# A gated residual block on one core: two head pairs and a quarter of the frames per step of the recurrence, r, k, v by way of DRAM, grams of two heads in turn

## The chip, the core and the metric

The kernel runs on one core of a Trainium2 chip. The metric is device time in microseconds of one execution; the runs of the kernel before took 2218.48 us in the median (2216.34 to 2221.33). The core has five engines that work beside each other, each in its own order: TensorE (PE; its weight loads are listed as PEld), VectorE (DVE), ScalarE (ACT), GpSimd (POOL) and SyncE (SP), which here issues all transfers. TensorE writes to PSUM, from where VectorE and ScalarE fetch its results.

## The reference

One layer over 1024 frames of 1024 channels, cut to what matters:

```
h    = RMSNorm(x);  P = h @ W_in             # r | k | v | glu | gate logits
r, k, v: each mixed with the frame before
w, a, g: low-rank functions of h             # decay, learning rate, gate
kk = normalised (k * k_k) per head;  k = k * (1 + (a - 1) * k_a)
# 16 heads of 64 channels, state S (64 x 64) per head, frame by frame
S_t = S_{t-1} diag(w_t) - (S_{t-1} kk_t) (kk_t a_t)^T + v_t k_t^T
o_t = S_t r_t
A    = (GroupNorm(o) + bonus(r, k, v)) * g
C    = swish(LayerNorm(causal depthwise conv, 31 taps, of the glu))
y    = sigmoid(gA) * (A @ W_A) + sigmoid(gC) * (C @ W_C)
x    = x + y @ W_out;  x = x + relu(RMSNorm(x) @ W1)^2 @ W2;  out = RMSNorm(x)
```

## The kernel before, in words

All data lies with channels on the partitions, 128 at a time, and frames along the free dimension, in halves of 512 (SEG). A large product is done as three products of float32r parts (high x high, high x low, low x high), 128x512 each; a unit of the combined projection is 48 of them. The weights come by DMA into `raw` and are split into `whi` (ScalarE) and `wlo` (VectorE or GpSimd).

**The recurrence** is done by chunks of 64 frames. Within a chunk it is matrix algebra; from chunk to chunk the state is handed on. Two heads of 64 channels fill the 128 partitions: a head pair p, of eight. A step i of 16 is one head pair and one half of the frames, 8 chunks. The parts of a step are generators:

- `prep` (L695) loads the decay (`sg`) and learning rate (`ta`), makes the scaled keys `bk`, the probes `pr` and the bonus. r, k, v of the pair are taken from SBUF, where the evacuation of the projection (`u_rkv`, L651) left them, three buffers each.
- `front` (L797), once for each four chunks: transposes `bk`, then makes the gram products `pg` of `bk` with `pr`: four for the first head (partitions 0 to 63), a tick, four for the second (64 to 127). ScalarE and VectorE copy them out, masked, to `lt`, `pl` and `mr`. The PSUM buffers `pg`, `pt`, `pv`, `pi`, `px` and so on share two banks.
- `invert` (L842): the inverse of I - L of each chunk, diagonal blocks of 16 by substitution on GpSimd after a way through DRAM (`scr_l`, `scr_x`, `scr_z`, `xz`), then blocks of 32 and 64 by small products (`pi`, `px`, `pt`, `pz`).
- `v_tm` (L774): transposes v into `sav` and `stv`, which then hold v beside places for the state.
- `chain` (L934): the chunks one after another, three groups of products a chunk, one a tick. First group: `pc` from `stv` and `pl`, and `po` from `stv` and `pr`; VectorE copies `pc` to `rsb`. Second group: `pc` from `rsb` and the inverse z; VectorE copies it to `sav`. Third group: `pc` from `sav` and `bkt`, and `po` from `sav` and `mr`; VectorE makes the next chunk's state, `pc` times the decay `wc` plus `stw`, where `stw` is the old state times the decay, made by ScalarE.
- `group_norm` (L986), after the chain of the step; its result goes to `a_d` in DRAM.

**The order.** Everything in this stage is traced by one loop of ticks, 24 (NT) for a step. At each tick every live generator is taken one stage further, then large products are traced until a running price of TensorE's work (`mm_price`) reaches the tick's number times 1.8 us (`large`), then some operations of the convolution on VectorE. `PLAN` (L1111) says at which tick of which step a generator starts. While the loop runs, TensorE, VectorE, ScalarE, GpSimd and SP keep exactly the order in which they are traced. The large products come from a queue: r, k, v of a pair when the last pair's are used, the glu, then the 16 gate units.

**The tail.** After the loop, 16 products of `g2t` with `tg` (the gate of A) follow, with up to 1.7 us of leftover gate products traced before each, and then the products with W_A, the merge and the feed-forward part. These last read nothing that the change touches.

Of the kernel before, what the change touches and what calls it, by code (L numbers as in the profile page):

```python
# [17 lines left out]
P = 128  # L18
T = 1024
NK = 8  # L20
SEG = 512
NSEG = 2
# [72 lines left out]
def tile_hybrid_block(ctx: ExitStack, tc: tile.TileContext, xT, win, wap, wcp, wop, wf1, wf2,  # L95
# [3 lines left out]
    class Ordered:  # L99
        """While on, the instructions of an engine keep the order in which they are traced;  # L100
        work: how long they take, in ns."""
# [58 lines left out]
    z_d = [dtile(f"z_d{i}", [P, T]) for i in range(NK)]  # L160
    al_d = [dtile(f"al_d{i}", [P, T]) for i in range(NK)]
    bn_d = [dtile(f"bn_d{i}", [P, T]) for i in range(NK)]
# [192 lines left out]
    def pick():  # L355
        """The first of the queue whose time has come."""
# [26 lines left out]
    def rms_scale(acc, eps):  # L383
        """acc [128, SEG], per-partition partial sums of squares, becomes 1/sqrt(mean + eps) on all partitions."""
# [1593 lines left out]
```

## Time and profile before

| | |
|---|---|
| runs, median (lowest to highest) | 2218.48 us (2216.34 to 2221.33) |
| profiled execution, its span | 2220.0 us |
| TensorE busy | 2075.3 us, 93%, 12806 records |
| VectorE busy | 1617.9 us, 73%, 2781 instructions |
| ScalarE busy | 1120.3 us, 50%, 2102 instructions |
| GpSimd busy | 898.0 us, 40%, 1026 instructions |
| transfers | 224.87 MB, mean 101 GB/s |

The profiled execution is one run, 1.5 us longer than the median of the others. A busy share is a mean over stages with different limits, so the stage that is changed is read by itself. TensorE's records of matrix products are pipelined and their ends are modelled: a busy time holds overlap, and the distance from one start to the next says what a product costs. A product of float32 operands has two records, so "x8" in a row is four products.

### The profile page before, as it was taken

What the parts mean: (1) busy time and instruction counts of PE and PEld (TensorE: products, weight loads), DVE (VectorE), ACT (ScalarE), POOL (GpSimd) and SP (SyncE); (2) the same over time, 40 slices, a digit from 0 to 9 for tenths busy, and PEclk for the clock granted to TensorE, in tenths of its full rate; (3) what the DMA queues carried; (4) which work ended last, traced back from release to release, by engine and by line L of the source; (5) the groups of instructions that cost most, each with busy time, mean ns of one, the idle gap of its engine ahead of it and who ended that gap; (6) DMA issues with size and microseconds to landing.
All of it is one profiled execution on the core that took longest, in us unless ns stands there. A gap on an engine that the chain in (4) does not pass through costs nothing. (4 is left out here: it accounts for less than half of the span.)

```text
span 2220.0 us, 35280 instructions
## 1 busy us (share of the span) xinstructions
PE 2075.3 (93%) x12806; PEld 1554.3 (70%) x12806; DVE 1617.9 (73%) x2781; ACT 1120.3 (50%) x2102; POOL 898.0 (40%) x1026
## 2 busy tenths in 40 slices
PE   6999999999999999999989989799899998889897
PEld 4757666767676666676666778577688876667686
DVE  8435889869778888898484987979432249998865
ACT  7454555555555555654323753455555555333323
POOL 4103333333333333342112245665545456566641
PEclk8999999999999999999999999999899999999999
DMA  5243222222222222232254355242433334233212
GB/s 180 90 158 79 62 73 53 80 65 78 78 66 79 72 81 72 74 87 82 70 178 159 128 170 163 95 137 93 169 105 114 105 106 151 91 95 105 85 49 76
DMA packets 223358, 224.87 MB, mean 101 GB/s; under 512 B 113488, under 2 KB 131408, under 8 KB 223184
## 3 DMA queue, kind: packets, MB, share of 16 engines
q1 hardware_dynamic: 223184, 222.62, 32.3%
q8 instruction: 101, 1.65, 0.3%
q14 instruction: 73, 0.60, 0.1%
HBM read 155.96 MB, written 66.60 MB: 100 GB/s over the span
## 5 line engine op out<-in xcount | busy, mean ns | idle before, releaser
L114 POOL TENSOR_TENSOR wlo<-raw,whi 128x512 fp32r<-128x512 f32 x258 | 369.4, 1434 | 698.9 <-ACT whi L114 640.1
L114 PE MATMUL g<-hhi,whi 128*128 128x512 f32 x912 | 402.9, 442 | 0.0
L114 PE MATMUL g<-hhi,wlo 128*128 128x512 f32 x912 | 363.4, 398 | 2.1 <-POOL wlo L114 1.5
L114 PE MATMUL g<-hlo,whi 128*128 128x512 f32 x912 | 364.8, 400 | 0.0
L114 ACT ACTIVATE whi<-raw 128x512 fp32r<-128x512 f32 x328 | 204.5, 625 | 222.4 <-PE g L114 73.0
L114 PEld LDWEIGHTS g<-hhi,whi 128*128 128x128 f32 x912 | 173.1, 190 | 52.4 <-issue 6.0
L114 PE MATMUL x<-place,whi 128*128 128x512 f32 x608 | 195.5, 403 | 14.8 <-DVE cmean L114 7.8
L114 PE MATMUL x<-a,whi 128*128 128x512 f32 x544 | 177.2, 408 | 33.3 <-ACT c L114 11.3
L114 PE MATMUL g<-place,whi 128*128 128x512 f32 x624 | 198.8, 399 | 7.6 <-ACT place L114 4.1
L114 PEld LDWEIGHTS g<-hhi,wlo 128*128 128x128 f32 x912 | 174.4, 191 | 44.5 <-POOL wlo L114 2.4
L114 PE MATMUL g<-a,whi 128*128 128x512 f32 x624 | 196.9, 397 | 5.7 <-DVE c L114 3.3
L114 PEld LDWEIGHTS g<-hlo,whi 128*128 128x128 f32 x912 | 174.1, 191 | 26.6 <-issue 1.9
L114 DVE TENSOR_TENSOR c<-c,g 128x512 f32<-128x512 f32 (+1 forms) x131 | 84.6, 650 | 94.8 <-PE g L114 94.6
L114 PEld LDWEIGHTS x<-a,whi 128*128 128x128 f32 x544 | 105.2, 196 | 63.0 <-ACT c L114 12.7
L114 PEld LDWEIGHTS x<-place,whi 128*128 128x128 f32 x608 | 115.1, 192 | 48.1 <-issue 6.2
L114 POOL TENSOR_TENSOR wlo<-s,whi 128x512 fp32r<-128x512 f32 x72 | 107.5, 1495 | 100.1 <-ACT whi L114 91.8
L114 PEld LDWEIGHTS g<-place,whi 128*128 128x128 f32 x624 | 118.2, 190 | 38.6 <-ACT place L114 5.0
L114 PEld LDWEIGHTS g<-a,whi 128*128 128x128 f32 x624 | 117.7, 190 | 35.7 <-DVE c L114 4.6
L114 POOL TENSOR_TENSOR tmpb<-lb,xb 64x15 f32<-64x15 f32 (+7 forms) x240 | 110.2, 459 | 79.3 <-DMA lb<-scr_l 63.2
L114 ACT ACTIVATE stw<-stv,wc 64x64 f32<-64x64 f32 x240 | 82.6, 344 | 97.7 <-DVE stv L114 94.2
L114 PE MATMUL g<-a,wlo 128*128 128x512 f32 x312 | 123.4, 396 | 5.6 <-POOL wlo L114 5.2
L114 PE MATMUL g<-place,wlo 128*128 128x512 f32 x312 | 123.6, 396 | 1.6 <-POOL wlo L114 1.6
(286 smaller groups left out, 4327.6 us busy)
## 6 DMA issues: line engine op xcount, KB each, us to landing
raw<-wf SPq DMA_DIRECT2D x128, 256.0 KB, 2.8
raw<-win SPq DMA_DIRECT2D x124, 256.0 KB, 3.1
f_d<-c SPq DMA_DIRECT2D x56, 256.0 KB, 2.0
fl<-f_d SPq DMA_DIRECT2D x46, 256.0 KB, 2.9
c<-f_d SPq DMA_DIRECT2D x18, 256.0 KB, 3.3
xt<-xT SPq DMA_DIRECT2D x16, 256.0 KB, 5.3
ga_d<-gt SPq DMA_DIRECT2D x16, 256.0 KB, 2.1
z_d<-za SPq DMA_DIRECT2D x16, 256.0 KB, 2.0
```

Of the source, the lines that this page charges most:

```text
L114: ins = f(*a, **k)
```

## The change

A step now takes two head pairs (`e` = 0, 1) and a quarter of the frames (QF = 256, four chunks). There are again 16 steps and 24 ticks a step, and the tiles of a step keep their sizes, since 2 x 256 frames stand where 512 stood. The state is handed on four times a step, for both pairs at once, two ticks from group to group.

- `u_rkv` stores r, k, v to DRAM; `prep` fetches them by quarters (`fetched`), one buffer each.
- Operations with a factor per channel are split in two, one for each pair: the square of k, `kk`, `ta`, `rkk`, the last one of the group norm, and the `a_d` store.
- In `front`, the gram products of both heads are traced in turn into two PSUM buffers taken at once.
- In `chain`, the state's old part enters the third group's sum by a product of the identity with `stv`, so ScalarE's `stw` goes, and VectorE multiplies the sum by the decay.
- The first two pairs' r, k, v and the first glu unit are made before the loop; later pairs' units come due at fixed ticks.

```diff
+    rkv_d = {n: [dtile(f"{n}_d{i}", [2, P, T]) for i in range(NK // 2)] for n in "rkv"}
-        rp = st.enter_context(tc.tile_pool(name="rp", bufs=3))
+        rp = st.enter_context(tc.tile_pool(name="rp", bufs=1))
...
-                    RKV[which, NSEG * p + s] = t
+                    sync.dma_start(rkv_d[which][p // 2][p % 2][:, s * SEG : (s + 1) * SEG], t)
+                    made.add((which, p, s))
...
+        def quarter(d, i):
+            return d[i // 4].rearrange("e p t -> p e t")[:, :, (i % 4) * QF : (i % 4 + 1) * QF]
+        def block(e, c):
+            return 4 * e + c
+        def fetched(which, i):
+            pp, u = divmod(i, 4)
+            need(which, 2 * pp, u // 2)
+            need(which, 2 * pp + 1, u // 2)
+            t = rp.tile([P, SEG], F32, tag=which, name=which)
+            sync.dma_start(two(t), quarter(rkv_d[which], i))
+            return t
...
-            k = RKV["k", i]
+            k = fetched("k", i)
             sg, ta = t2k("sg"), t2k("ta")
-            sync.dma_start(sg, z_d[p][:, sl])
-            sync.dma_start(ta, al_d[p][:, sl])
+            sync.dma_start(two(sg), quarter(z_d, i))
+            sync.dma_start(two(ta), quarter(al_d, i))
+            yield
             sq = t2k("sq")
-            act.activation(sq, k, AF.Square, scale=v("kk", p))
+            for e, p in enumerate(P2):
+                act.activation(two(sq)[:, e], two(k)[:, e], AF.Square, scale=v("kk", p))
...
-            for h in range(2):
-                rows = slice(64 * h, 64 * h + 64)
-                pg = mp.tile([P, 4, P], F32, tag="m", name="pg")
-                for j in range(4):
-                    pe.matmul(pg[:, j, :], bk[rows, 4 * q + j, :, :].rearrange("p a t -> p (a t)"),
+            pgs = [mp.tile([P, 4, P], F32, tag="m", name="pg") for h in range(2)]
+            for j, b in enumerate(blocks):
+                for h, rows in enumerate((H0, H1)):
+                    pe.matmul(pgs[h][:, j, :], bk[rows, b, :, :].rearrange("p a t -> p (a t)"),
                               pr[rows, j, :, :].rearrange("p a t -> p (a t)"), start=True, stop=True)
-                yield
...
+            for c in range(4):
+                q, cc = divmod(c, 2)
...
+                for e in pairs:
+                    for h in range(2):
+                        pe.matmul(ps1[hr[h], e], Q["pl"][:, h, 2 * e + cc, :], stv[:, h, 2 * e + cc, :],
+                                  start=True, stop=True)
+                rs = sp.tile([P, 2, 64], F32, tag="rsb", name="rsb", bufs=2)
+                dve.tensor_copy(rs, ps1)
...
-                    stw = sp.tile([P, 64], F32, tag="stw", name="stw", bufs=2)
-                    for h in range(2):
-                        act.activation(stw[hr[h]], Q["stv"][hr[h], h, j, :], AF.Copy,
-                                       scale=wc[hr[h], c, 0:1])
...
+                if not (u == 3 and c == 3):
+                    for e in pairs:
+                        for h in range(2):
+                            pe.matmul(ps3[hr[h], e], ident[:, 64 * h : 64 * h + 64], stv[:, h, 2 * e + cc, :],
+                                      start=True, stop=False)
+                            pe.matmul(ps3[hr[h], e], Q["bkt"][:, 2 * e + cc, 64 * h : 64 * h + 64],
+                                      sav[:, 2 * e + cc, 64 * h : 64 * h + 64], start=False, stop=True)
...
                     for h in range(2):
-                        dve.scalar_tensor_tensor(out=nstv[hr[h], h, nj, :], in0=ps3[hr[h]],
-                                                 scalar=wc[hr[h], c, 0:1], in1=stw[hr[h]],
-                                                 op0=ALU.mult, op1=ALU.add)
+                        dve.tensor_tensor(out=nstv[hr[h], h, nc_:4:2, :], in0=ps3[hr[h]],
+                                          in1=wc[hr[h], c:8:4, :].to_broadcast([64, 2, 64]), op=ALU.mult)
...
-        PLAN = [(1, 2, prep), (24, 0, group_norm), (15, 2, front0), (24, 2, front1), (35, 2, v_tm), (29, 2, invert)]
+        PLAN = [(0, 2, prep), (24, 0, group_norm), (14, 2, front0), (24, 2, front1), (34, 2, v_tm), (28, 2, invert)]
...
+        while ("v", 1, 1) not in made:
+            large(pe.work + TICK)
+            conv_ops(2, dve.work + TICK * DSHARE)
```

What this makes of TensorE's order is shown at three places. The first is the gram products of one front, with buffer numbers. Before, each head's four stand together, into one buffer, with a group of the chain between the heads:

```order
L114 MATMUL l_10937<-hsh_10842,bonr_156 128x512
L114 MATMUL l_10937<-hsl_10844,bonr_156 128x512
L114 MATMUL pg_10942<-pr_10885,bk_10789 128x128 x4
L114 MATMUL pc_10950<-stv_10194,pl_9869 64x64 x2
L114 MATMUL po_10492<-pr_9844,stv_10194 64x64 x2
L114 MATMUL pg_10965<-pr_10885,bk_10789 128x128 x4
```

After, the heads' eight alternate between two buffers:

```order
L115 MATMUL l_5705<-hsh_5662,bonr_156 128x512
L115 MATMUL l_5705<-hsl_5664,bonr_156 128x512
L115 MATMUL pg_5709<-pr_5665,bk_5299 128x128
L115 MATMUL pg_5710<-pr_5665,bk_5299 128x128
L115 MATMUL pg_5709<-pr_5665,bk_5299 128x128
L115 MATMUL pg_5710<-pr_5665,bk_5299 128x128
L115 MATMUL pg_5709<-pr_5665,bk_5299 128x128
L115 MATMUL pg_5710<-pr_5665,bk_5299 128x128
L115 MATMUL pg_5709<-pr_5665,bk_5299 128x128
L115 MATMUL pg_5710<-pr_5665,bk_5299 128x128
```

Numbers 5709 and 5710 are the two heads' buffers: what was two groups of four is one of eight.

The second place is the third group of a chunk on TensorE, with what stands around it. Before, two products into `pc` and two into `po`:

```order
L114 MATMUL g<-hhi,wlo 128x512
L114 MATMUL pc<-sav,bkt 64x64 x2
L114 MATMUL po<-mr,sav 64x64 x2
L114 MATMUL l<-hsh,bonr 128x512
L114 MATMUL l<-hsl,bonr 128x512
```

After, for two pairs (`cst` holds the identity):

```order
L115 MATMUL g<-hhi,wlo 128x512
L115 MATMUL pc<-stv,cst 64x64
L115 MATMUL pc<-sav,bkt 64x64
L115 MATMUL pc<-stv,cst 64x64
L115 MATMUL pc<-sav,bkt 64x64
L115 MATMUL pc<-stv,cst 64x64
L115 MATMUL pc<-sav,bkt 64x64
L115 MATMUL pc<-stv,cst 64x64
L115 MATMUL pc<-sav,bkt 64x64
L115 MATMUL po<-mr,sav 64x64 x4
```

The product of the identity and the one with `bkt` that follows it go to the same half of the partitions; then comes the other half. The first and second groups have four products of each kind where they had two.

The third place is the tail on TensorE, from the last large products on h (`hhi`, `hlo`) to the first with W_A (`a`). Before, nine large products stand between one product of `g2t` and the next, for the first nine:

```order
L114 MATMUL g<-hlo,whi 128x512
L114 MATMUL g<-hhi,wlo 128x512
L114 MATMUL g<-tg,g2t 128x512
L114 MATMUL g<-hhi,whi 128x512
L114 MATMUL g<-hlo,whi 128x512
L114 MATMUL g<-hhi,wlo 128x512
```

After, there are none left:

```order
L115 MATMUL g<-hhi,wlo 128x512
L115 MATMUL l<-hsh,bonr 128x512
L115 MATMUL l<-hsl,bonr 128x512
L115 MATMUL g<-tg,g2t 128x512 x15
L115 MATMUL cm<-cmean_12306,cst 128x512
L115 MATMUL g<-tg,g2t 128x512
L115 MATMUL g<-a_12331,whi 128x512 x2
```

In the whole order, the runs of small products between large ones number 393 before and 245 after; behind the last product of the chain stand 269 large products on h before, 81 after.

## Rows read from the trace of the kernel before

**Rows 1.** Windows: length, busy us of PE, PEld, DVE, ACT, POOL, clock, DMA share, GB/s.

```profile
0.00:231.00 231.00, 207.90 (x924) 148.83 (x924) 130.41 (x239) 124.05 (x210) 50.14 (x74) 0.94 0.39 126
231.00:1135.60 904.60, 871.56 (x7681) 619.84 (x7680) 742.99 (x1582) 492.79 (x1045) 314.72 (x580) 0.99 0.27 73
1135.60:1218.60 83.00, 78.40 (x301) 57.19 (x300) 49.05 (x69) 28.77 (x46) 15.91 (x12) 0.98 0.61 199
1218.60:2220.00 1001.40, 917.44 (x3906) 728.40 (x3904) 695.48 (x894) 474.72 (x804) 517.19 (x360) 0.97 0.34 113
```

**Rows 2.** Timeline of PE, chain groups: start us, us, operation, records, idle before.

```profile
515.84 0.39 PE L114 MATMUL g<-hhi,wlo 128*128 128x512 f32 x1
516.16 0.33 PE L114 MATMUL pc<-rsb,z 64*64 64x64 f32 x4
516.42 0.50 PE L114 MATMUL g<-hhi,whi 128*128 128x512 f32 x1
...
531.77 0.39 PE L114 MATMUL g<-hhi,wlo 128*128 128x512 f32 x1
532.09 0.34 PE L114 MATMUL pc<-sav,bkt 128*64 128x64 f32 x4
532.26 0.29 PE L114 MATMUL po<-mr,sav 128*64 128x64 f32 x4
532.47 0.50 PE L114 MATMUL g<-hhi,whi 128*128 128x512 f32 x1
532.81 0.40 PE L114 MATMUL g<-hlo,whi 128*128 128x512 f32 x1
533.05 0.39 PE L114 MATMUL g<-hhi,wlo 128*128 128x512 f32 x1
...
533.73 0.39 PE L114 MATMUL g<-hhi,wlo 128*128 128x512 f32 x1
534.05 0.34 PE L114 MATMUL pc<-stv,pl 128*64 128x64 f32 x4
534.32 0.33 PE L114 MATMUL po<-pr,stv 64*64 64x64 f32 x4
534.58 0.49 PE L114 MATMUL g<-hhi,whi 128*128 128x512 f32 x1
```

**Rows 3.** Timeline of PE, the gram products of one head and what follows.

```profile
519.04 1.16 PE L114 MATMUL pg<-pr,bk 64*128 64x128 f32 x8
520.13 0.34 PE L114 MATMUL pc<-stv,pl 128*64 128x64 f32 x4
```

**Rows 4.** Timeline of PE, products of the inverse, both heads in turn.

```profile
504.76 1.15 PE L114 MATMUL pi<-xz,lm 64*64 64x64 f32 x32
505.84 0.34 PE L114 MATMUL pc<-sav,bkt 128*64 128x64 f32 x4
506.00 0.29 PE L114 MATMUL po<-mr,sav 128*64 128x64 f32 x4
506.59 0.69 PE L114 MATMUL px<-lm,xz 32*32 32x32 f32 x32 [0.30 <-ACT lm L114]
```

**Rows 5.** Tile sg: ns min/median/max, first and last start us, landing.

```profile
L114 SPq DMA_DIRECT2D sg<-z_d x14: 423/464/730, 224.5 to 960.2; - x14
L114 DVE TENSOR_TENSOR_SCAN cum<-scanmask,sg x14: 1214/1215/1225, 238.9 to 969.7; 128x512 f32<-128x512 bf16 x14
DMA to landing us min/median/max: 3.6/4.7/6.1
```

**Rows 6.** Timeline of PE, the tail: last product of the chain, first with W_A.

```profile
1135.29 0.34 PE L114 MATMUL po<-mr,sav 128*64 128x64 f32 x4
...
1186.68 1.02 PE L114 MATMUL g<-tg,g2t 128*128 128x512 f32 x2
...
1218.61 1.03 PE L114 MATMUL g<-a,whi 128*128 128x512 f32 x2
```

More of the change, by code (lines that the diff above doesn't have):

```diff
@@ L748, in prep @@
             rkk = t2k("rkk")
-            dve.scalar_tensor_tensor(out=rkk, in0=r, scalar=v("rk", p), in1=k2, op0=ALU.mult, op1=ALU.mult)
+            for e, p in enumerate(P2):
+                dve.scalar_tensor_tensor(out=two(rkk)[:, e], in0=two(r)[:, e], scalar=v("rk", p),
+                                         in1=two(k2)[:, e], op0=ALU.mult, op1=ALU.mult)
             yield
@@ L767, in prep @@
             yield
-            need("v", i)
             bn = rkk
-            dve.tensor_tensor(out=bn, in0=ps, in1=RKV["v", i], op=ALU.mult)
+            dve.tensor_tensor(out=bn, in0=ps, in1=E["v"], op=ALU.mult)
             yield
-            sync.dma_start(bn_d[p][:, sl], bn)
+            sync.dma_start(quarter(bn_d, i), two(bn))
         def v_tm(i):
-            vv = RKV["v", i]
+            vv = D[i]["v"]
             pv = mp.tile([P, 4, P], F32, tag="m", name="pv")
@@ L778, in v_tm @@
                 pe.transpose(pv[:, w, :], vv[:, w * P : (w + 1) * P], ident)
-            done.add(("v", i))
             yield
@@ L939, in chain @@
             hr = [H0, H1]
+            pairs = range(2)
             po = op.tile([P, NCH, 64], F32, tag="o", name="po")
[L941 to L942 removed]
+            for c in range(4):
+                q, cc = divmod(c, 2)
                 Q = E["q"][q]
[L944 removed]
+                stv, sav = Q["stv"], Q["sav"]
+                pc = chp.tile([P, 3, 2, 64], F32, tag="c", name="pc")
                 ps1, ps2, ps3 = pc[:, 0], pc[:, 1], pc[:, 2]
[L946 to L958 removed]
@@ L959, in chain @@
+                yield
+                yield
+                for e in pairs:
+                    for h in range(2):
+                        pe.matmul(ps2[hr[h], e], z[hr[h], block(e, c), :], rs[hr[h], e], start=True, stop=True)
+                for h in range(2):
+                    dve.tensor_copy(sav[0:64, cc:4:2, 64 * h : 64 * h + 64], ps2[hr[h]])
                 yield
-                for h in range(2):
-                    pe.matmul(ps2[hr[h]], z[hr[h], c, :], rs[hr[h]], start=True, stop=True)
@@ L962, in chain @@
-                dve.tensor_copy(Q["sav"][0:64, j, 0:64], ps2[0:64])
-                dve.tensor_copy(Q["sav"][0:64, j, 64:128], ps2[64:128])
                 yield
-                if not last:
-                    for h in range(2):
-                        pe.matmul(ps3[hr[h]], Q["bkt"][:, j, 64 * h : 64 * h + 64],
-                                  Q["sav"][:, j, 64 * h : 64 * h + 64], start=True, stop=True)
-                    if c < NCH - 1:
-                        nq, nj = divmod(c + 1, 4)
+                if not (u == 3 and c == 3):
+                    for e in pairs:
+                        for h in range(2):
+                            pe.matmul(ps3[hr[h], e], ident[:, 64 * h : 64 * h + 64], stv[:, h, 2 * e + cc, :],
+                                      start=True, stop=False)
+                            pe.matmul(ps3[hr[h], e], Q["bkt"][:, 2 * e + cc, 64 * h : 64 * h + 64],
+                                      sav[:, 2 * e + cc, 64 * h : 64 * h + 64], start=False, stop=True)
+                    if c < 3:
+                        nq, nc_ = divmod(c + 1, 2)
@@ L1015, in group_norm @@
             bn = sp.tile([P, SEG], F32, tag="gns", name="gnb")
-            sync.dma_start(bn, bn_d[p][:, sl])
+            sync.dma_start(two(bn), quarter(bn_d, i))
             yield
@@ L1019, in group_norm @@
             yield
-            dve.scalar_tensor_tensor(out=o, in0=o, scalar=v("lxg", p), in1=bn, op0=ALU.mult, op1=ALU.add)
+            for e in range(2):
+                dve.scalar_tensor_tensor(out=two(o)[:, e], in0=two(o)[:, e], scalar=v("lxg", 2 * (i // 4) + e),
+                                         in1=two(bn)[:, e], op0=ALU.mult, op1=ALU.add)
             yield
-            sync.dma_start(a_d[p][:, sl], o)
+            for e in range(2):
+                sync.dma_start(a_d[2 * (i // 4) + e][:, (i % 4) * QF : (i % 4 + 1) * QF], two(o)[:, e])
         convs = []
@@ L1089, in conv, with need @@
             done.add(("c_d", p))
-        queue.append((passed(), [u_rkv(0, "k"), decay_and_a, u_rkv(0, "r"), u_rkv(0, "v"), gate_lora]))
-        for p in range(NK):
-            if p:
-                i = NSEG * p + NSEG - 1 - 3
-                queue += [(passed((n, i)), [u_rkv(p, n)]) for n in "krv"]
-        queue += [(lambda p=p: p == 0 or ("conv", p - 1) in done, glu_units(p)) for p in range(NK)]
+        queue.append((passed(), [u_rkv(0, "k"), u_rkv(1, "k"), decay_and_a] + glu_units(0) +
+                      [u_rkv(e, x) for x in "rv" for e in range(2)] + [gate_lora]))
+        tick = [0]
+        for pp in range(1, NK // 2):
+            for j, (x, e) in enumerate((x, e) for x in "krv" for e in range(2)):
+                due = NT * (4 * pp - 4) + 15 * j
+                queue.append((lambda due=due: tick[0] >= due, [u_rkv(2 * pp + e, x)]))
+        queue += [(lambda p=p: ("conv", p - 1) in done, glu_units(p)) for p in range(1, NK)]
         queue += [(passed(), [gate_unit(n, (1,) if n < EARLY else (0, 1))]) for n in range(2 * NK)]
         advance(8)
-        def need(which, i):
-            while (which, i) not in RKV:
+        def need(which, p, s):
+            while (which, p, s) not in made:
                 next(G)
```

98 lines of the change are left out of this document (51 added, 47 removed).

## The prediction

> **What bounds the kernel now.** I read the table of stages first, because the change touches one stage only. The span falls into four pieces: a start, the recurrence, a short tail, and the feed-forward part [rows 1]. In the recurrence, 904.6 us long, TensorE is busy for 871.6 us, so 33.0 us are idle. VectorE is busy 743 us (82%), ScalarE 493 us, GpSimd 315 us, and the DMA engines 27%. TensorE bounds this stage and the others almost as closely. Nothing else may be said to bound it as long as VectorE's share stays below TensorE's. So I look for what the change does to the time that TensorE needs, and then for what it does to the 33 us.
>
> A busy TensorE hides two prices. The timeline of TensorE shows them as start-to-start distances, which I trust more than modelled ends. Large products (128x512) follow one another every 0.24 us (532.81 to 533.05) [rows 2]. Each excursion into small products costs more than the products do. I take the distance from the last large product before it to the first one after it, less 0.235 us:
>
> - the second group of a chunk, two products (pc from rsb and z): 516.42 - 515.84 - 0.235 = 0.345 us [rows 2];
> - the third, four products (pc from sav and bkt, po from mr and sav): 532.47 - 531.77 - 0.235 = 0.465 us;
> - the first, four products in two shapes (pc from stv and pl, po from pr and stv): 534.58 - 533.73 - 0.235 = 0.615 us.
>
> The first large product after an excursion then takes 0.34 us instead of 0.235 us (532.47 to 532.81) [rows 2], so leaving costs 0.105 us per excursion. The gram products of one head, four of them, take 520.13 - 519.04 = 1.09 us, or 0.27 us each [rows 3]. Sixteen 64x64 products that alternate between the two heads (pi) take 505.84 - 504.76 = 1.08 us, or 0.0675 us each [rows 4]. That is a quarter of a gram product at half its columns, thus twice as fast per column: two heads in different halves of the array's rows run together there.
>
> **The change part by part.** There are 16 steps before and after, of 24 ticks each. Before, a step has 8 chunks of one pair, so 128 chunk turns; after, 4 chunks of two pairs, so 64 turns of twice the products.
>
> *Fewer, longer groups.* The price of one more pair of products within a group is 0.135 us (eight pairs of pi in 1.08 us) [rows 4] to 0.17 us (the distance from pc to po in the third group) [rows 2]; I take 0.14 us, the value for two heads side by side. Per turn:
> first group 0.615 + 2 x 0.14 = 0.895 us against 2 x 0.615 = 1.23: 0.335 us less;
> second group 0.345 + 0.14 = 0.485 against 0.69: 0.205 us less;
> third group: another po pair (0.14), and eight products into pc where there were two, since the product of the identity with stv takes the place of ScalarE's stw. Were all eight to pair, they would add 3 x 0.14 = 0.42 us. Were none to, a product of 64 columns alone is half a gram product (0.135 us), and they would add 8 x 0.135 - 0.14 = 0.94 us. In the new order two products for the same half of pc follow each other, then two for the other half, so only neighbours across the border can pair: I take 0.61 us, between the two. The group then costs 0.465 + 0.14 + 0.61 = 1.215 us against 0.93: 0.285 us more.
> Sum: 0.255 us less per turn, x 64 = 16 us less (28 us less to 5 us more).
>
> *Fewer exits.* In the program's order TensorE has 393 excursions before and 245 after. 148 x 0.105 = 15.5 us less. That the other groups (px, pt of the inverse, the transposes) now stand partly alone is in this count.
>
> *Grams in pairs.* 256 gram products in 64 groups of four: 64 x 1.09 = 70 us. After, 32 groups of eight that alternate between heads. If two run together, a group of eight costs what four cost now, 1.09 us: 35 us less. If not, nothing is gained; a loss would need a price for changing the bank, and no row has one. The heads stand in different halves of the rows as in pi, but unlike there both write all 128 partitions, so the rows do not decide it. I take the pairing, because the nearest rows are those of pi, and keep 0 as the other end.
> The Trainium skill, TensorEngine Tiling (Array Packing), section Gotcha 1: PSUM Pressure, says that row tiles must write to different banks and cannot use one bank at once. The new order meets that, and the old one could not have gained by alternation alone; no row of before shows two row halves over the same columns.
>
> *The identity products' weight loads.* In the third group of before, two products over all 128 rows, loads included, take 0.17 us [rows 2], so their loads hide.
> The Trainium skill, TensorE: Matmul & The Clock Gate, Part 3, The mechanism, says that weight loads overlap running products only where the row groups differ, else only by way of the background buffer; here all eight share all rows. By that rule the eight would not pair at all, the 0.61 us become 0.94 us, and the sum below shrinks by 60 x 0.33 = 20 us. The row speaks against it.
>
> *VectorE and ScalarE.* The chain's VectorE operations halve in number (five a turn) and double in width; three per step are split in two. ScalarE loses stw. Neither engine is the bound, so I cost this at nothing; the cover is TensorE's 871.6 us against 743 us. It would cost something only if VectorE's work came above some 840 us.
>
> *Stalls.* A group of the chain now has two ticks for the answer of VectorE, where it had one. Of the 33.0 us idle I take 10 us as gone (0 to 20). Something new comes late: in about nine places px now follows pi with no product between. Today px starts 506.59 - 505.84 = 0.75 us after pi, with the third group between them and still 0.30 us of waiting for ScalarE's lm [rows 4]. Alone it waits the 0.75 us: 9 x 0.75 = 7 us more.
>
> *r, k, v through DRAM.* 48 stores and 48 loads of 256 KB, and one more a_d store per step, all behind each other on SP's queue with the weight loads. The first reader is ScalarE's square of k, one tick (904.6/384 = 2.4 us) after the load; behind it on ScalarE stands bkt's copy, which frees a PSUM buffer, and TensorE waits for that. Today SP issues the load of sg 9.5 to 14.4 us before VectorE's scan reads it, which stands two ticks (4.7 us) behind in the order [rows 5]. So SP runs 5 to 10 us ahead, plus the one tick, 7 us at the least, against 4.7 us from issue to landing (6.1 us at most). I cost it at nothing; that lead hides it.
>
> *Start and tail.* The first two pairs' r, k, v are made before the loop: the same large products, earlier. They are then missing at the end: after the last product of the chain there are 81 large products on h instead of 269. Before, that tail takes 1218.61 - 1135.29 = 83.3 us [rows 6], of which 269 x 0.235 = 63.2 us are large products. After, 19.0 us of them are left beside the other 20 us. The group norm of the last step must pass under these; the filler is thinner, the fifteen tg products stand in a row, and the last ones wait for it. I put that at 3 us (0 to 44).
>
> Sum: -16 - 15.5 - 35 - 10 + 7 + 3 = -66.5 us. On the profiled span of 2220.0 us this gives 2153.5 us. The median of the runs shown, 2218.48 us, stands 1.5 us under that span, so I predict 2152 us. The bounds of the terms without the tail's far end, which is a rival, reach from -28 - 15.5 - 35 - 20 + 7 + 0 = -91.5 us to +5 - 15.5 - 35 + 0 + 7 + 10 = -28.5 us, grams paired.
>
> **The rivals.**
>
> *The grams don't pair.* For it: both write the same columns of the array, which no row shows done at once. Against it: pi. Then 35 us fewer are saved: 2187 us.
>
> *The tail is not covered.* If the last group norm takes as long as now, the tail stays 83.3 us although 44 us of its large products went elsewhere: 2152 + 41 = 2193 us. Against it: the group norm of before was paced by large products and by VectorE's last convolution, which now ends inside the loop.
>
> *More is saved.* The eight products pair fully and most stalls go, the lower bound above: 2220 - 91.5 - 1.5 = 2127 us.
>
> *Slower: the loads come late.* If the stores of r, k, v hold SP back (a store waits for VectorE, and everything on the queue behind it waits too) and its lead is lost, each of the three loads of a step is seen whole by its reader: 16 x 3 x 4.7 = 226 us, so 2152 + 226 = 2378 us. From 66.5/16 = 4.2 us of TensorE idle per step on the kernel is slower than before, which is about one load seen whole. Against it: SP's lead [rows 5].
>
> **How the numbers follow.** Forecast 0.62, grams unpaired 0.13, tail uncovered 0.09, more saved 0.09, loads late 0.07. The forecast's own range is 2135 to 2175 us. The range 2120 to 2198 us takes in the unpaired grams, the open tail and the larger gain; the loads and a combination of losses are left out. A difference of 0.2% (4.4 us) is what a measurement of this kernel can tell from none. Faster 0.89: all but the loads, and a little of the two middle rivals together. Same 0.04, slower 0.07.
>
> **What would show it.** Right: gram groups of eight in about 1.1 us, their records starting in pairs; the three groups of a turn near 0.9, 0.5 and 1.2 us; the last product of the chain near 1110 us instead of 1135 us (1218.6 - 66.5 - 42 for the tail); the tail near 40 us; the feed-forward part unchanged at 1001 us. Wrong: gram groups of 2.1 us; third groups above 1.5 us; TensorE idle behind ScalarE's square of k or behind PSUM copies in every step; large idle time among the tg products.

## The result: slower by 1.6%, and the profile after

The changed kernel takes 2255.4 us (median; 2249.4 to 2259.3 in four runs), the kernel before 2217.4 us beside it: ratio 1.0156, 95% interval 1.0127 to 1.0186. The forecast was 2152 us, range 2120 to 2198. It was wrong in sign.

The first view to read is the same table of stages as in [rows 1], for the kernel after (length, busy time of PE, PEld, DVE, ACT, POOL, granted clock, DMA share, GB/s):

```profile
0.00:305.20 305.20, 276.69 (x1233) 203.20 (x1233) 173.64 (x313) 141.47 (x240) 58.77 (x83) 0.96 0.38 128
305.20:1198.40 893.20, 792.00 (x8031) 599.65 (x8030) 660.71 (x1270) 444.75 (x848) 311.48 (x567) 0.94 0.34 96
1198.40:1247.30 48.90, 38.10 (x124) 22.70 (x120) 28.12 (x42) 19.57 (x30) 10.22 (x8) 0.90 0.71 239
1247.30:2247.60 1000.30, 918.31 (x3906) 729.62 (x3904) 699.01 (x894) 474.53 (x803) 518.74 (x360) 0.97 0.34 113
```

Start, tail and feed-forward part are nearly as forecast. The start is 74 us longer, for 309 large products that now stand there (the prediction gave it no number of its own). The tail takes 48.9 us (forecast about 42), the last stage 1000.3 us, 1.1 us less than before. The loss is in the second row. Forecast for it: 805 us (last product of the chain near 1110). Measured: 893.2 us. TensorE is busy for 792.0 us, 17 us more than the 775 us that 805 less 30 of idle time leave; and it idles for 101.2 us where 33.0 us stood before and 30 were forecast. Its mean granted clock is 0.94 instead of 0.99: the clock records add up to 116 us at half speed (1.2 GHz) in this stage, against 20.5 us before.

The unit prices of the prediction hold, away from the waits. The timeline of TensorE after, with the second group (`pc<-rsb,z`), eight grams and the third group, answers to [rows 2, 3]:

```profile
537.48 0.40 PE L115 MATMUL g<-hhi,wlo 128*128 128x512 f32 x1
537.81 0.45 PE L115 MATMUL pc<-rsb,z 64*64 64x64 f32 x8
538.19 0.50 PE L115 MATMUL l<-hsh,bonr 128*128 128x512 f32 x1
538.53 0.40 PE L115 MATMUL l<-hsl,bonr 128*128 128x512 f32 x1
538.85 1.16 PE L115 MATMUL pg<-pr,bk 64*128 64x128 f32 x16
539.95 0.49 PE L115 MATMUL g<-hhi,whi 128*128 128x512 f32 x1
...
541.22 0.40 PE L115 MATMUL g<-hhi,wlo 128*128 128x512 f32 x1
541.55 0.34 PE L115 MATMUL pc<-stv,cst 128*64 128x64 f32 x4
541.72 0.29 PE L115 MATMUL pc<-sav,bkt 128*64 128x64 f32 x4
541.83 0.34 PE L115 MATMUL pc<-stv,cst 128*64 128x64 f32 x4
541.95 0.33 PE L115 MATMUL pc<-sav,bkt 128*64 128x64 f32 x4
542.07 0.45 PE L115 MATMUL po<-mr,sav 128*64 128x64 f32 x8
542.45 0.49 PE L115 MATMUL g<-hhi,whi 128*128 128x512 f32 x1
```

Eight grams take 1.10 us to the next start, as four did before. The second group costs 538.19 - 537.48 - 0.235 = 0.475 us (forecast 0.485), the third 542.45 - 541.22 - 0.235 = 0.995 us (forecast 1.215), the first 0.855 us (forecast 0.895, a stretch not shown). So away from the half clock the work fell by as much as the sum said, and a little more (in numbers: an estimate, under *The clock* below). What came back is waiting, and time at half clock. TensorE's three longest waits in the recurrence, first before, then after (what was waited for, us in total, times, longest):

```profile
PE pc L114 <- DVE stv L114: 13.7, 26, 1.2
PE pi L114 <- DMA xz<-scr_x: 6.6, 8, 1.6
PE pc L114 <- DVE sav L114: 4.0, 7, 1.2
```

```profile
PE pi L115 <- DMA xz<-scr_x: 29.6, 13, 6.1
PE pt L115 <- DVE bk L115: 19.1, 10, 2.8
PE pc L115 <- DVE stv L115: 18.2, 16, 2.1
```

The largest is pi, the first product of the inverse, for the load of xz. One such place on TensorE's timeline answers to [rows 4]; these rows follow one another without a gap in the list:

```profile
679.16 1.16 PE L115 MATMUL pg<-pr,bk 64*128 64x128 f32 x16
682.20 0.45 PE L115 MATMUL pc<-stv,pl 128*64 128x64 f32 x8 [1.88 <-DVE stv L115]
682.58 0.45 PE L115 MATMUL po<-pr,stv 64*64 64x64 f32 x8
686.42 0.44 PE L115 MATMUL pi<-xz,lm 64*64 64x64 f32 x2 [3.39 <-DMA xz<-scr_x]
687.34 1.97 PE L115 MATMUL pi<-xz,lm 64*64 64x64 f32 x30 [0.47 <-DMA xz<-scr_x]
689.24 0.79 PE L115 MATMUL g<-hhi,whi 128*128 128x512 f32 x1
689.83 0.63 PE L115 MATMUL g<-hlo,whi 128*128 128x512 f32 x1
```

TensorE waits 1.88 us for stv, then 3.39 us for xz. When it resumes, 15 products of pi take 1.97 us where 16 took 1.15, and the second large product behind them starts 0.59 us after the first instead of 0.34 [rows 2]: the clock is at half. The windows of the kernel after around it show that (same columns as above):

```profile
660.00:683.60 23.60, 19.45 (x173) 14.60 (x172) 20.21 (x39) 17.89 (x33) 18.13 (x32) 1.00 0.31 89
683.60:690.50 6.90, 3.60 (x35) 2.89 (x35) 2.00 (x6) 0.60 (x1) 0.00 (x0) 0.51 0.87 239
```

What pi waits for is a path outside TensorE. SP's queue in the same step (start of each transfer, its issue in us):

```profile
655.85 1.28 SPq L115 DMA_DIRECT2D scr_l<-lt  x2
...
658.98 0.59 SPq L115 DMA_DIRECT2D lb<-scr_l  x1
...
681.03 0.58 SPq L115 DMA_DIRECT2D scr_x<-xb  x1
...
683.62 1.27 SPq L115 DMA_DIRECT2D xz<-scr_x  x2
```

lt goes to DRAM and comes back as lb, GpSimd substitutes until 681.0, xb goes to DRAM and comes back as xz: 30.6 us from 655.85 to pi at 686.42. From the second store of lt to pi it is 33.1 us in the mean of the 16 steps after (29.1 to 36.9) and 32.9 us before (29.5 to 35.4); to the last xz load's issue, 30.0 and 29.5 us. Its length did not change. In the program's order pi stands 14 ticks behind the last lt, before and after. Before, 14 ticks are 14 x 2.36 = 33 us, just enough. With the forecast stage of 805 us a tick is 2.1 us, and 14 are 29 us. At that pace TensorE would arrive some 4 us early in each of 16 steps (an estimate from mean ticks). The experiments test this.

### The profile page after: what moved, and what is told of

Its sections match the earlier page's. It is cut to its first block, busy times and chain, and to the rows that moved or that the text cites. A ratio compares the mean times of both kernels' runs of the same rounds, so it can differ in the third digit from the quotient of the medians.

```text
span 2247.6 us, 35965 instructions
## 1 busy us (share of the span) xinstructions
PE 2025.1 (90%) x13286; PEld 1555.2 (69%) x13286; DVE 1561.5 (69%) x2517; ACT 1080.3 (48%) x1920; POOL 899.2 (40%) x1018
## 3 DMA queue, kind: packets, MB, share of 16 engines
q1 hardware_dynamic: 253648, 247.79, 35.1%
## 5 line engine op out<-in xcount | busy, mean ns | idle before, releaser
L115 PE MATMUL g<-hhi,whi 128*128 128x512 f32 x912 | 392.2, 430 | 0.2 <-ACT whi L115 0.2
L115 PE MATMUL g<-hhi,wlo 128*128 128x512 f32 x912 | 370.6, 406 | 2.9 <-POOL wlo L115 1.2
L115 PE MATMUL g<-hlo,whi 128*128 128x512 f32 x912 | 371.3, 407 | 0.0
L115 PEld LDWEIGHTS g<-hhi,whi 128*128 128x128 f32 x912 | 178.0, 195 | 47.5 <-issue 4.3
L115 PE MATMUL x<-place,whi 128*128 128x512 f32 x608 | 195.0, 402 | 12.6 <-DVE cmean L115 7.8
L115 POOL TENSOR_TENSOR tmpb<-lb,xb 64x15 f32<-64x15 f32 (+7 forms) x240 | 109.2, 455 | 46.0 <-DMA lb<-scr_l 29.5
L115 PE MATMUL x<-place,wlo 128*128 128x512 f32 x304 | 121.7, 400 | 0.9 <-POOL wlo L115 0.9
```

The source lines that it names most:

```text
L115: ins = f(*a, **k)
```

## Experiments

**Two theories.** *Short ticks*: the ticks got shorter, the inverse's path did not, so TensorE waits at pi, and its clock falls. *Loads*: the stores of r, k, v hold SP's queue, k comes late, and all behind it. For the second speaks that ScalarE's square of k does wait after:

```profile
ACT sq L115 <- DMA k<-k_d: 23.0, 6, 4.8
```

**k early.** In the kernel after, k's load is issued about ten ticks sooner, into a second buffer:

```diff
-            k = fetched("k", i)
+            k = K.pop(i) if i in K else fetched("k", i)
...
             probe(0)
+            if i + 1 < NK * NSEG:
+                K[i + 1] = fetched("k", i + 1)
```

> The kernel after, with one change: the load of k for the next step is issued at the end of this step's preparation (stage 14, about ten ticks before its first reader, into a second buffer) instead of one tick ahead. Theory of the loads (the stores of r, k, v hold SP's queue back, so ScalarE's square of k waits and all that hangs on it comes late): ScalarE's wait of 27.6 us on k goes below 4 us, TensorE's wait of 19.1 us on pt from VectorE's bk goes below 6 us, and the time falls by 15 to 30 us, to 2225 to 2240 us. Theory of the short ticks (TensorE's tick got shorter than paths that are counted in ticks, such as the inverse, and these stay): ScalarE's wait goes too, but TensorE meets the other waits sooner (pi on xz, 30.3 us, grows), and the time stays within 10 us of 2255 us.

Measured: 2252.2 us, ratio to before 1.0147 (1.0119 to 1.0175), not to be told from after. The recurrence takes 901.7 us. The wait for k is gone from ScalarE, and TensorE's waits are what they were:

```profile
PE pi L115 <- DMA xz<-scr_x: 30.5, 13, 6.2
PE pc L115 <- DVE stv L115: 20.6, 16, 2.6
PE pt L115 <- DVE bk L115: 18.0, 10, 2.8
```

The loads theory falls for k: its wait is real, and taking it away gains nothing that the runs can tell.

**pi two ticks later.** In the kernel after, pi and the inverse's products behind it stand 16 ticks behind lt:

```diff
-W_XZ = 2
+W_XZ = 4
```

> The kernel after, with the products on the inverse's blocks (pi and what follows it) two ticks later in the order, 16 instead of 14 ticks after the second half of lt. Theory of the short ticks: TensorE's 30.3 us of waits for xz go below 8 us, since 16 ticks of 2.1 to 2.3 us are 34 to 37 us and the path takes 31 to 34 us; the time falls by 15 to 30 us, to 2225 to 2240 us. Theory of the loads: the waits for pt and stv, which it puts behind late loads of k, stay, and TensorE's idle time only moves there: within 10 us of 2255 us.

Measured: 2198.5 us, ratio 0.9907 (0.9877 to 0.9938): 57 us less than after, twice what I expected, and faster than before. The stage's row, then TensorE's waits:

```profile
308.40:1142.70 834.30, 770.47 (x8064) 582.55 (x8064) 650.48 (x1269) 448.16 (x852) 306.13 (x567) 0.98 0.36 103
```

```profile
PE pt L115 <- DVE bk L115: 13.4, 10, 2.4
PE pc L115 <- DVE stv L115: 11.8, 13, 1.9
PE pi L115 <- DMA xz<-scr_x: 11.3, 8, 3.7
```

58.9 us of the stage are gone: 37.4 us of idle time (101.2 to 63.8), of which pi's wait is 18.3, and 21.5 us of busy time, with the time at half clock down from 116 to 41 us. The same products run; they run fast more of the time. That is the part that I had not expected. And ScalarE's wait for k, 23.0 us in after, is gone too, though k is loaded no sooner here:

```profile
ACT sq L115 <- DMA k<-k_d: 1.0, 1, 1.0
```

The late k was thus not the stores' doing alone, since the same stores stand on SP's queue here; it came and went with pi's place.

**Grams cheaper in the order's price list.** In the kernel after:

```diff
+        if r.dtype == F32 and l.shape[0] <= 64 and width(l) == 128:
+            n *= 2.7
-        if r.dtype == F32:
+        elif r.dtype == F32:
```

> The kernel after, with the price that the order counts for a gram product cut from 213 to 144 ns (the trace has 1.16 us for eight), so that about 75 more large products stand within the recurrence, most of them just behind the grams, and only a handful is left behind it. Theory of the short ticks and of the clock that goes with them: the ticks with grams become longer, TensorE idles less (101 us to 70 or less) and its clock is granted at half for fewer than 116 us (70 or so); 17 us of work move from the tail into the recurrence, and the time falls by 20 to 40 us, to 2215 to 2235 us. Theory of the loads: the idle time stays at 90 to 100 us, the recurrence is longer by the 17 us that the tail is shorter, and the time stays within 10 us of 2255 us, or is longer where the tail is now uncovered.

Measured: 2273.4 us, 18 us slower than after. What the theory of short ticks said here failed, and of the two theories the other came nearer (idle time of 90 to 100 us, a longer time where the tail is uncovered). This run does not speak for short ticks; the runs that vary the place of pi, above and below, do. The stage takes 919.0 us, idle 100.5 us, half clock 119.5 us; pi's wait for xz is 39.8 us. The added products came on top and filled no idle time: the 14 ticks hold only one of a step's two groups of grams, and the path was itself somewhat longer in this run (means of 16 steps from the second scr_l to the last xz load's issue: 30.9 us against 30.0). The tail, with 42 products instead of 124, still takes 45.7 us: it is set by its own waits, not by its products.

**Paired grams alone, in the kernel before.** The loop over heads moves inside the loop over blocks, and both banks are taken at once:

```diff
-                for j in range(4):
-                    pe.matmul(pg[:, j, :], bk[rows, 4 * q + j, :, :]...
-                yield
+            for j in range(4):
+                for h, rows in enumerate((H0, H1)):
+                    pe.matmul(pgs[h][:, j, :], bk[rows, 4 * q + j, :, :]...
+            yield
```

> The kernel before, with one part of the change alone: the gram products of both heads in one tick, alternating between two PSUM banks. If pairing is worth what it seemed (32 groups more of four at 1.09 us that vanish, 35 us) and nothing new waits: 2183 us. Theory of the short ticks: half or more of it comes back as waits for the inverse's path (pi on xz, 6.6 us before, 15 to 25 us here): 2195 to 2210 us. Rival, the two PSUM buffers: with both taken at once the next product into them waits for VectorE's and ScalarE's reads, and the time is not below 2217 us.

Measured: 2217.4 us, ratio 0.9997 (0.9979 to 1.0015). The stage's row:

```profile
231.50:1130.70 899.20, 842.41 (x7681) 592.96 (x7680) 742.80 (x1584) 493.24 (x1045) 317.68 (x580) 0.99 0.27 73
```

TensorE is 29 us less busy than before (871.6) and 24 us more idle (56.8 against 33.0). Pairing is real, and nearly all of it is waited away. The time is the one that the rival of the two PSUM buffers gave (not below 2217 us), and a part is of its kind: pi waits 7.3 us for mr, VectorE's read that frees the buffer. The rest is not: TensorE's waits for sav rose from 4.0 to 17.1 us, and pi waits 8.7 us for xz. The path to the last xz load's issue is itself longer here, 32.2 us in the mean against 29.5; why is not settled.

**The substitution in fewer ticks, pi where it was**, and **with pi two ticks later**. N_SUB, the steps of GpSimd's substitution per tick, goes from 2 to 4; W_XZ to 6 in the first run (shown) and to 8 in the second, so that pi stands 14 and 16 ticks behind lt.

```diff
-N_SUB = 2
+N_SUB = 4
-W_XZ = 2
+W_XZ = 6
```

> The kernel after, with GpSimd's 15 substitution steps of the inverse handed out in three ticks instead of seven (N_SUB 4), and the four ticks put behind the loads of xz, so that pi stays 14 ticks behind lt. Less of GpSimd's other work, a weight split that waits for ScalarE, then stands between the substitution steps. It shortens the path that pi waits for, where the run before moved pi. Theory of the path (pi comes too soon for it): waits for xz 30.3 to below 15 us, half clock 116 to below 80 us, time 2255 to 2205 to 2230 us. Rival, the place (the gain of pi two ticks later came from its place in the order, away from the grams and the third group, where the clock falls): the waits for xz may shrink, the half clock stays near 116 us, and the time above 2240 us.

> Both: the substitution in three ticks, and pi 16 ticks behind lt. Theory of the path: nothing is left to wait for, xz below 3 us (11.3 us with pi later alone), half clock 41 us or less, time 2198 to about 2180 to 2192 us. If what is left of the idle time (pt on bk 13.4, stv 11.8 us) takes over at once, it stays at 2195 to 2200 us.

Measured: 2281.8 us (ratio 1.0285, 1.0240 to 1.0330) and 2213.9 us (0.9978, 0.9957 to 1.0000): 26 us slower than after, 15 us slower than pi later alone. Both expectations missed, and the first run shows what came in the way. Its waits of TensorE, VectorE and SP:

```profile
PE pi L115 <- issue: 32.7, 11, 6.7
PE pc L115 <- DVE stv L115: 23.9, 16, 4.2
```

```profile
DVE rkk L115 <- DMA v<-v_d: 26.9, 9, 5.6
```

```profile
SPq L115 <- POOL xb L115: 185.0, 16, 22.1
```

xz is no longer late (its load is issued about 25 us behind scr_l in most steps). But the store scr_x now stands four ticks earlier in SP's queue and waits there for GpSimd: 185.0 us, where after has 97.8. The load of v stands behind it, and VectorE, which never waited for v in after, waits 26.9 us. Behind that on VectorE stand the four reads of the grams, which free the PSUM buffer that pi needs. Its timeline, with pi starting at 635.71:

```profile
634.02 0.69 DVE L115 TENSOR_TENSOR rkk<-l,v 128x512 f32<-128x512 f32 x1 [2.06 <-DMA v<-v_d]
634.75 0.43 DVE L115 TENSOR_TENSOR pl<-pg,cst 64x256 f32<-64x256 f32 x1
635.19 0.42 DVE L115 TENSOR_TENSOR mr<-pg,cst 128x256 f32<-128x256 f32 x1
```

pi starts 0.1 us after the first mr. The view names no releaser for it ("issue"); that it is the buffer is read from these rows, not shown by a run. A second thing changed: TensorE's large products wait 15.0 us for weight splits of GpSimd (`wlo`, 1.2 us in after), which now stand behind the denser substitution. The runs do not part the two. In the second run VectorE waits 35.1 us for v. So my rival of late loads does exist as a mechanism, with v instead of k, once SP is held longer. It is not what slowed the kernel after, where VectorE does not wait for v. Since the shorter path brought these waits with it, the two runs do not test the theory of the path.

**Later front and k early, on top of pi later**, and **later front alone**:

```diff
-        PLAN = [(0, 2, prep), (24, 0, group_norm), (14, 2, front0), ...
+        PLAN = [(0, 2, prep), (24, 0, group_norm), (15, 2, front0), ...
```

> pi 16 ticks behind lt, and with it k loaded ten ticks ahead and the first half's transposes and grams (pt, pg) one tick later, two ticks behind the last of bk instead of one. Theory of the short ticks: TensorE's wait for bk (13.4 us) goes below 4 us and the time falls by another 8 to 15 us, to 2183 to 2190 us. Theory of the loads, now that the inverse is out of the way: k early is worth what it was not worth before, and the same numbers would follow from it; ScalarE's wait for k tells how much of it. Rival: the waits move on to stv and rsb (17 us) and the time stays at 2195 to 2202 us.

> pi 16 ticks behind lt, and of the two further edits of the run before only the later front (pt and grams of the first half one tick later), with k loaded one tick ahead as in the changed kernel. Theory of the short ticks: the gain of that run came from the front, so 2183 to 2190 us again. Theory of the loads: it came from k, so 2195 to 2200 us, with ScalarE's waits for k back at 20 us or more and TensorE's wait for bk above 10 us.

Measured: 2185.4 us (0.9856, 0.9817 to 0.9894) with both, 2188.4 us (0.9857, 0.9826 to 0.9888) with the front alone. The front gains about 10 us over pi later alone, TensorE's wait for bk falls from 13.4 us to below 3 us. That k early adds nothing here says little: without it ScalarE waits only 1.8 us for k in this order.

**Pairing undone where pi is later.** The two loops change places (for h, then for j), both banks still taken at once:

```diff
-            for j, b in enumerate(blocks):
-                for h, rows in enumerate((H0, H1)):
+            for h, rows in enumerate((H0, H1)):
+                for j, b in enumerate(blocks):
```

> pi 16 ticks behind lt, and the eight gram products of a group head by head, so that neighbours are of the same head and bank: the pairing alone undone. If the pairing is worth what eight gram products cost less (32 groups x 1.09 us = 35 us at most) where TensorE is the bound: 2198 + 25 to 35 = 2223 to 2233 us, gram groups of 2.1 to 2.2 us. Theory of the short ticks: where ticks are short a part is hidden in waits, 2208 to 2223 us. If alternation is worth nothing: 2198 us and groups of 1.16 us.

Measured: 2194.9 us (0.9899, 0.9867 to 0.9930), the same as paired, where I expected 2208 us or more if alternation is worth anything. A gram group there, and the product behind it:

```profile
564.45 1.71 PE L115 MATMUL pg<-pr,bk 64*128 64x128 f32 x16
566.08 0.50 PE L115 MATMUL g<-hhi,whi 128*128 128x512 f32 x1
```

Eight take 1.64 us to the next start in the median, 1.09 us when they alternate. TensorE is 17.5 us more busy (788.0 against 770.5 us, and 32 x 0.55 = 17.6), the stage only 9 us longer (843.3 against 834.3), and the totals do not differ: in the profiled runs the start is 10.9 us shorter (297.5 against 308.4), and whether that has to do with the edit is not known. Of the 35 us that I gave to alternation, half comes from standing together. The single records say how (two a product, read from the traces): alternating, they start in pairs 6 ns apart, a pair every 0.11 us; head by head, one starts every 0.11 us, but for a few pairs where the heads meet.

**Paired grams and pi one tick later, in the kernel before** (W_XZ 3, the last place that its order allows).

> The kernel before with the gram products of both heads in one tick, alternating (which alone changed nothing: TensorE 29 us less busy, 24 us more idle), and with the inverse's products one tick later, 15 ticks behind lt; that is the last place that the order of before allows. Theory of the path: a part of the 29 us comes out, since 15 ticks are 2.3 us more for the path; pi's waits for xz and mr go from 16 to below 6 us, and the time from 2217 to 2200 to 2210 us. Rival: the waits of the chain itself (sav, stv: 30 us with pairing) are what pays for the pairing, and the time stays at 2213 to 2220 us.

Measured: 2207.0 us, ratio 0.9927 (0.9899 to 0.9955). The stage takes 884.2 us (899.2 with pairing alone), idle 48.0 us, half clock 3.4 us. pi no longer waits for xz (0.5 us) or mr; the chain's wait for sav stays (21.9 us). The profiled run took 2197.4 us, 10 us below the median, so the stage's 15 us are the favourable end. A part of what pairing is worth seems to come out as soon as pi is not in the way; that pi one tick later without pairing would not gain as much in this kernel was not run.

**One tick, in both kernels.** With W_XZ 3 in after, and W_XZ 1 in before:

> The kernel after with pi 15 ticks behind lt (14 in after, 2255 us; 16 in the run with pi two later, 2198 us). Pi then stands in a tick that holds no group of the chain, a tick behind the first group; at 14 it stands with the first group, at 16 with the second. Theory of the path: one tick more gives the path 2.1 to 2.3 us a step, so a good half of the 57 us comes back, 2218 to 2232 us, with waits for xz of 15 to 25 us (30.3 and 11.3 us at 14 and 16) and half clock between 116 and 41 us. Rival, the place: away from the first group and the grams all of it comes back, 2195 to 2205 us, though the waits for xz stay above 15 us.

> The kernel before with pi 13 ticks behind lt instead of 14, nothing else: its ticks are 2.36 us long, so the path (31 to 34 us) has 30.7 us instead of 33. Theory of the path: the kernel before falls off the same edge, pi's waits for xz rise from 6.6 us to 25 us or more, half clock from 20 us to 50 us or more, and the time from 2219 to 2240 to 2260 us. Rival (the loss is peculiar to the changed order, with its denser groups and its loads through DRAM): within 8 us of 2219 us.

Measured: 2216.2 us (0.9987, 0.9966 to 1.0008) and 2268.7 us (1.0217, 1.0191 to 1.0242). The first is 2 us below what the theory of the path gave and 11 us above what the rival, pi's place, gave; the second is 9 us above the theory's upper end. pi's waits in the two:

```profile
PE pi L115 <- DMA xz<-scr_x: 18.3, 10, 4.7
```

```profile
PE pi L114 <- DMA xz<-scr_x: 14.3, 10, 4.6
```

In order of ticks between lt and pi:

| kernel | ticks | time, us | pi waits for xz, us | half clock, us |
|---|---|---|---|---|
| before | 13 | 2268.7 | 14.3 | 92 |
| before | 14 | 2218 | 6.6 | 20 |
| after | 14 | 2255.4 | 29.6 | 116 |
| after | 15 | 2216.2 | 18.3 | 68 |
| after | 16 | 2198.5 | 11.3 | 41 |

Each tick taken away costs 18 to 51 us, in both kernels, whichever group pi stands beside. Meanwhile the path from the second store of lt to the last xz load's issue stays at 29.4 to 30.0 us in the means of these five runs, while a step's mean tick goes from 2.17 to 2.47 us. So it is the path that pi runs into, not pi's place. The kernel before stood at the same edge, one tick from a loss larger than that of the change. Its wait rose less than I expected (14.3 instead of 25 us), its time more: of 42.7 us more in the stage, 19.1 are idle time and 23.6 busy time, with 92 us at half clock instead of 20:

```profile
233.10:1180.30 947.20, 895.10 (x7681) 640.91 (x7680) 721.81 (x1556) 491.99 (x1044) 310.14 (x580) 0.95 0.26 70
```

**Two more on the way down.** On top of pi later, k early and the later front: the group norm's load of gnb issued when the group norm begins, into a buffer of its own; then also less convolution per tick for VectorE (DSHARE, in the second run only).

```diff
             o = D[i]["o"]
+            bn = sp.tile([P, SEG], F32, tag="gnb", name="gnb")
+            sync.dma_start(two(bn), quarter(bn_d, i))
...
-            bn = sp.tile([P, SEG], F32, tag="gns", name="gnb")
-            sync.dma_start(two(bn), quarter(bn_d, i))
...
-DSHARE = 0.75
+DSHARE = 0.65
```

> pi 16 ticks behind lt, k ten ticks ahead, the front one tick later, and the group norm's load of the bonus (gnb from bn_d) issued when the group norm begins instead of three ticks before VectorE reads it. VectorE waits 13.4 us for that load in the run without this, and TensorE 12.6 us for VectorE's mr behind it. Theory of the short ticks (a DRAM detour counts where its wait stands in the queue of an engine that a short tick waits for): VectorE's wait goes to below 2 us, pi's wait for mr below 6 us, and 2185 becomes 2172 to 2180 us. Rival: TensorE meets the chain's own waits (stv, rsb, sav: 28 us) instead, and the time stays at 2182 to 2188 us.

> As the run with the bonus loaded early, and with less of the convolution given to VectorE in a tick (DSHARE 0.65 instead of 0.75), so that its answers to the chain come sooner. Theory of the short ticks: the waits for stv, rsb and sav, 28 us, fall to 15 us or less, the time by about 8 to 12 us below that run, near 2165 to 2172 us. Rival, the convolution that is left at the end: what VectorE does not do within the recurrence it does behind it, the tail grows from 49.6 to 60 us or more, and the time is not lower than that run's.

Measured: 2188.2 us (0.9858, 0.9830 to 0.9885) and 2180.3 us (0.9815, 0.9795 to 0.9835). The first gains nothing: VectorE's wait for gnb (13.4 us) is gone, pi's for mr falls from 12.6 to 0.8 us, and pi waits 6.7 us for xz instead. The second gains 8 us: the stage falls from 830.0 to 819.8 us, the waits for stv, rsb and sav from 29.1 to 21.9 us, and the tail grows from 46.8 to 54.3 us, since VectorE finishes the convolution there. The gain is at the low end of what the first side said, with half of the fall in waits that it asked for; the tail grew by 7.5 us where the other side said 10 or more, and did not eat the gain. It is the fastest version, 1.8% below before.

## Why the prediction was wrong, step by step

*The step that failed is the stalls.* "Of the 33.0 us idle I take 10 us as gone (0 to 20)" and 7 us for px (4.1 us measured): I forecast 30 us of idle time and got 101.2. The stage took 88 us more than forecast: 71 us of idle time and 17 us of busy time, and the busy time holds some 30 us of half clock (below) over work that came out smaller than said. I read the 33 us as something that faster work can only reduce. But [rows 4] show one pi without a wait, and not by how much it escapes one. The waits for xz before, 6.6 us in eight places, show that pi stood at the edge, and its input comes by a path that TensorE does not speed up. The order's 14 ticks were 33 us of cover. The terms that I booked as gains (-16, -15.5, -35) shorten these ticks, so they take the cover away. What will be late next, I asked of ScalarE's lm and not of xz. It should be asked of every wait that is close to zero.

*The clock.* No term had it. 95 us more at half clock (116 against 20.5) go with the waits; in the pairs of runs that differ by pi's place alone, busy time rises by 0.29 us (21.5/75) and 0.33 us (23.6/71.7) per us at half clock, so about 30 us of the loss are of this kind, an estimate from these two ratios. That is why a tick costs more than its wait. What sets the clock back I do not settle: each of the 17 falls in after comes with waits of TensorE of 1 to 6 us, during one or shortly after, but not every such wait brings one (2.3 us near 392 us does not).

*Fewer, longer groups*: right, and 0.22 us per third group better than said. The eight products into pc, each over all 128 rows, take 542.07 - 541.55 = 0.52 us, 0.065 us each, as fast as pi: the end that the prediction called all paired (0.42 us more), not the 0.61 us between the two.
The Trainium skill, TensorE: Matmul & The Clock Gate, Part 3, The mechanism, let me work out that these would not pair; the trace shows them as dense as those that alternate between row halves.

*Grams in pairs*: right that two run together, half right on what that is worth. Eight take what four took, and their records start in pairs, as the prediction's sign asked; but alternation is worth 17.6 us and standing together the other half. In the kernel before it lowers busy time by 29 us, where the grams and their 32 exits were booked at 38.

*r, k, v through DRAM*: zero was right, the reason was not. I said that SP's lead of 5 to 10 us hides the load. In six steps ScalarE waits for k, 23.0 us in all, so the lead is not always there. The wait is harmless: loading k early changed nothing to be told. And it goes with the stalls: 1.0 us of it is left when pi is two ticks later.

*VectorE at nothing*: too low. Of TensorE's waits for bk and stv, 37.3 us after, 25.2 us remain when pi is two ticks later, and moving the front or taking convolution away gains 8 to 10 us each. A busy share of 74% did not mean an answer within two ticks.

*Tail*: 48.9 us for about 42, a miss of 7; its floor is near 46 us.

*The rivals*: unpaired grams did not come. Loads late was the only rival on the right side, with 0.07, for a mechanism that did not decide. That the gain is lost to a path whose length the change leaves as it is was not among them.

## What to carry to other kernels

In an order that counts distances in ticks, a cut in the work shortens every distance. So before booking the gain, list the paths that leave the engine (DRAM, GpSimd), measure each in microseconds, and divide by the new tick; a path with no wait may have no slack. When it falls short, move its end in the order first, and then measure the change. And a store that waits in a queue that keeps its order delays the loads behind it (v, in the run with the tighter substitution): putting it earlier in that queue can cost more than it brings.

## What the runs showed of the hardware that I had not expected

Waits of 1 to 6 us among small products go with a granted clock of 0.5 for 3 to 14 us, though not each of them; 17 such stretches are 116 of 893 us in after. Gram products (64 rows of contraction, 128 x 128 out, fp32) over different row halves and different banks run two at a time though both write all 128 partitions: 1.09 us for eight when alternating, 1.64 us head by head.
The Trainium skill, TensorEngine Tiling (Array Packing), section Gotcha 1: PSUM Pressure, asks for different banks; here both orders use two banks, and alternation alone makes the 0.55 us.
